# DeltaNet mixer of a two-layer DiT: loop order written as slots with TensorE's order pinned, q and k norms as per-token scales

## The chip, the core and the metric

One NeuronCore of a Trainium2 chip runs the whole program. The metric is the device time of one execution in microseconds (us).

## The reference

Two layers over 768 tokens (256 context, 512 image) of width 1024, batch 1, all in fp32. Layer 0 mixes with a gated DeltaNet, layer 1 with gated linear attention (GLA), and each has a feed-forward network with squared ReLU. Shift, scale and gate vectors come from a conditioning vector ("ada"). The change touches the DeltaNet alone:

```python
qkv = silu(short_conv(h @ w_qkv, conv_w))            # 5 taps
q = l2_normalize(q) * 128 ** -0.5 ; k = l2_normalize(k)   # per token, 8 heads of 128
# 16 value heads; per direction d (forward, backward), chunk by chunk, state s:
m = where(strict, beta_i * (k_i . k_j) * decay_ij, 0)
u, w = solve(eye + m, [v * beta, k * beta * exp(G)])
v_new = u - w @ s
o = (q * exp(G)) @ s + (q k^T * decay) @ v_new
s = s * exp(G_last) + (k * exp(G_last - G))^T @ v_new
# readout: rms_norm(o_fwd + o_bwd) * silu(z) @ w_out
```

## The kernel before, in words

Activations lie with features on the partitions and the 768 tokens along the free axis. The kernel takes chunks of 128 tokens, six in all. The eight key heads are worked one after the other; one key head with its two value heads is called a head pair here (g = 0 to 7).

**Dense products.** `dense` (line 215) multiplies a 1024x128 weight block into all tokens. Operands are split into a high and a low fp32r part, so each of the eight k steps is six matmuls: three products (`dstep`, line 208), each on 256 and on 512 columns. The weights arrive by DMA in two halves (`weights`, line 195); ScalarE casts the high part (line 204) and GpSimd subtracts the low part (line 205). A head pair has six such jobs: k, q, two v, two z. Layer 0's output product `dn_wo` has eight for its first half, inside the loop.

**Per head pair.** `conv_tile` (401) evacuates a job, applies five taps (one on ScalarE, four on VectorE, line 414) and SiLU. `l2n` (427) normalises q and k over the 128 features: a square on ScalarE, a product with a matrix of ones, Ln and Exp on ScalarE over 128x770, and a multiply on VectorE. `prep` (473) makes decay matrices E, products k k^T and k q^T, the matrices N and A (lines 487 to 494), then inverts the triangular systems: 32x32 blocks by a chain of 30 dependent pairs on VectorE (514 to 520), and larger blocks by small matmuls (`ZM`, lines 538 and 549; `LC`, line 563). `seq` (571) runs the recurrence: six steps in two directions. Each of the twelve turns has the products with S (593, 616), R on VectorE (596), U R (599), a copy x on ScalarE (601), Kt x and A x (607, 618), the new S (614) and the sum into oN. `zproj` (637) and `onorm` (651) make the gate, the output norm and the store.

**What sets the order.** The loop at lines 676 to 702 emits `prep(g+1)`, `seq(g)`, `zproj(g)`, `proj(g+2)`, `vproj(g+1)` and `onorm(g)` one after the other. The framework plans every engine's order when the program is built: an instruction goes as early as its planned inputs, buffers and place in the program allow. So matmuls of `seq(g)` and of later dense jobs stand interleaved, in an order that nobody wrote. On the chip each engine then runs its list in that order and waits on semaphores. SyncE's queue issues the loads and stores. PSUM is divided into tags: two banks "c" (`prep`), one "n", two "s" (`seq`), and three banks for dense outputs.

## Time and profile before

| what | value |
|---|---|
| median of 3 runs | 2505.73 us (2499.26 to 2512.78) |
| profiled execution | 2505.4 us |
| its span, first to last instruction | 2503.4 us |
| mean granted TensorE clock | 0.962 |

The profile is of that one execution. Busy time is the union of an engine's instructions; matmuls are pipelined and their ends are modelled, so a TensorE that shows as busy need not run at its rate. The rate is read from the starts of successive matmuls. PEld is the weight load. The clock is granted at one of two levels, 1.2 and 2.4 GHz, shown as 0.50 and 1.00, or as a mean.

### The profile page before, as it was taken

How to read it: one execution, taken by the hardware profiler on the slowest of the kernel's cores; microseconds unless marked ns; L12 is line 12 of the kernel's file. 1: busy time of each engine (PE TensorE's matmuls, PEld its weight loads, DVE VectorE, ACT ScalarE, POOL GpSimd, SP SyncE). 2: the span in 40 equal slices, each digit the busy share in tenths (PEclk: the TensorE clock that was granted, in tenths of full speed). 3: DMA queues.
4: the chain of work that ended last, by engine and by line, in shares of the span. 5: the costliest groups of instructions: out<-in, count | busy, mean ns of one | idle time of the engine just before them, and what ended most of it. 6: DMA issues, size and time to landing. Idle time of an engine off the chain costs nothing. (4 is left out here: it accounts for less than half of the span.)

```text
span 2503.4 us, 34922 instructions
## 1 busy us (share of the span) xinstructions
PE 2322.1 (93%) x12984; PEld 1939.7 (77%) x12984; DVE 1582.9 (63%) x2571; ACT 1135.1 (45%) x2053; POOL 938.0 (37%) x864
## 2 busy tenths in 40 slices
PE   7889889988999999899899999999899999899999
PEld 4668768777878878677688888888688777688887
DVE  5586796968778786439878797881575754311111
ACT  4654546373737464342431414132565644533432
POOL 1234353535344443544233333333142234244443
PEclk7988899999999999999999999999999999999999
DMA  6110010111111011266234333331111124133332
GB/s 233 49 51 30 22 51 30 51 35 51 47 34 56 30 56 37 70 231 206 81 119 131 122 127 125 120 122 60 44 44 39 52 76 131 53 98 98 96 98 98
DMA packets 107306, 206.60 MB, mean 83 GB/s; under 512 B 12032, under 2 KB 12544, under 8 KB 107136
## 3 DMA queue, kind: packets, MB, share of 16 engines
q1 hardware_dynamic: 106848, 203.31, 24.9%
q8 instruction: 103, 1.69, 0.3%
q10 hardware_dynamic: 288, 1.05, 0.1%
q14 instruction: 67, 0.55, 0.1%
HBM read 190.68 MB, written 13.63 MB: 82 GB/s over the span
## 5 line engine op out<-in xcount | busy, mean ns | idle before, releaser
L75 POOL TENSOR_TENSOR wl<-wr,wh 128x512 fp32r<-128x512 f32 x419 | 572.7, 1369 | 1076.5 <-ACT wh L204 982.9
L204 ACT CAST wh<-wr 128x512 fp32r<-128x512 f32 x452 | 279.2, 620 | 749.9 <-PE d L98 683.5
L98 PE MATMUL d<-hh,wh 128*128 128x256 f32 (+1 forms) x1856 | 595.8, 370 | 20.1 <-ACT hh L261 14.2
L98 PE MATMUL d<-hh,wl 128*128 128x256 f32 (+1 forms) x1856 | 578.7, 362 | 8.0 <-POOL wl L75 7.9
L98 PE MATMUL d<-hl,wh 128*128 128x256 f32 (+1 forms) x1856 | 582.0, 363 | 1.0 <-DVE hl L263 1.0
L98 PEld LDWEIGHTS d<-hh,wh 128*128 128x128 f32 x1856 | 354.9, 193 | 75.4 <-ACT hh L261 18.1
L98 PEld LDWEIGHTS d<-hh,wl 128*128 128x128 f32 x1856 | 352.5, 193 | 54.0 <-POOL wl L75 10.4
L98 PEld LDWEIGHTS d<-hl,wh 128*128 128x128 f32 x1856 | 353.2, 193 | 49.5 <-DVE hl L263 3.4
L75 DVE TENSOR_TENSOR avp<-avw,cB 128x512 f32<-128x512 f32 x256 | 232.4, 936 | 99.2 <-DMA avw<-ada_t 97.0
L98 PE MATMUL d<-gh,wh 128*128 128x512 f32 (+1 forms) x768 | 232.5, 357 | 0.0
L98 PE MATMUL d<-gl,wh 128*128 128x512 f32 (+1 forms) x768 | 231.0, 356 | 1.1 <-DVE gl L75 1.1
L98 PE MATMUL d<-gh,wl 128*128 128x512 f32 (+1 forms) x768 | 231.3, 356 | 0.0
L78 DVE SCALAR_TENSOR_TENSOR xT<-d,mods,xT 128x256 f32<-128x256 f32 (+1 forms) x120 | 75.6, 657 | 202.0 <-PE d L98 202.0
L98 PEld LDWEIGHTS d<-gl,wh 128*128 128x128 f32 x768 | 144.4, 188 | 24.2 <-DVE gl L75 1.7
L98 PEld LDWEIGHTS d<-gh,wh 128*128 128x128 f32 x768 | 144.4, 188 | 22.0
L98 PEld LDWEIGHTS d<-gh,wl 128*128 128x128 f32 x768 | 144.5, 188 | 21.3
L75 POOL TENSOR_TENSOR U<-Y,cm 128x256 f32<-128x256 f32 x96 | 81.1, 849 | 210.2 <-PE s L98 146.2
L75 DVE TENSOR_TENSOR gl<-ft,gh 128x768 fp32r<-128x768 f32 (+1 forms) x64 | 52.6, 822 | 168.1 <-ACT gh L773 168.1
L189 DVE TENSOR_REDUCE mods<-avp 128x1 f32<-128x1024 f32 x128 | 156.1, 1219 | 4.0
L78 DVE SCALAR_TENSOR_TENSOR cv<-rp,convw,cv 128x770 f32<-128x770 f32 x128 | 141.0, 1101 | 26.3 <-ACT cv L412 25.1
L605 POOL TENSOR_SCALAR Kt<-Kn,tailb 128x128 f32<-128x128 f32 x160 | 121.3, 770 | 80.3 <-ACT Kn L443 42.7
L98 PE MATMUL d<-oh,wh 128*128 128x256 f32 (+1 forms) x320 | 97.9, 365 | 14.1 <-ACT wh L204 6.0
(269 smaller groups left out, 3823.2 us busy)
## 6 DMA issues: line engine op xcount, KB each, us to landing
wr<-ffn SPq DMA_DIRECT2D x256, 256.0 KB, 2.8
avw<-ada_t SPq DMA_DIRECT2D x128, 256.0 KB, 3.2
aw<-ada_w SPq DMA_DIRECT2D x64, 256.0 KB, 4.1
wr<-dn_qkv SPq DMA_DIRECT2D x64, 256.0 KB, 2.8
wr<-dn_z SPq DMA_DIRECT2D x32, 256.0 KB, 2.8
wr<-dn_wo SPq DMA_DIRECT2D x32, 256.0 KB, 3.2
oD<-of SPq DMA_DIRECT2D x16, 384.0 KB, 3.6
ol<-oD SPq DMA_DIRECT2D x16, 384.0 KB, 3.5
```

Of the source, the lines that this page charges most:

```text
L75: (eng or self.dve).tensor_tensor(o, a, b, op=op)
L78: self.dve.scalar_tensor_tensor(o, a, s, b, op0=op0, op1=op1)
L98: pe.matmul(out, lhsT, rhs, start=start, stop=stop, skip_group_check=True)
L189: dve.reduce_sum(mods[:, l, part, m, s:s + 1], p, axis=mybir.AxisListType.X)
L204: act.copy(wh, r)
L605: pool.tensor_scalar(Kt[:, hh], Kn[:, c], tailb[:, c, d, r0 + hh:r0 + hh + 1], None, op0=MUL)
```

## The change

The DeltaNet loop is rewritten as Python generators that are advanced slot by slot while the program is built. In each slot, in this order: one third of a turn of `seq` (a turn is three slots: S products, R and the previous turn's Kt x and A x; U and Kt for the next turn; U R and x); one k step (six matmuls) of the dense stream; one step of every side generator (conv with one tap a slot, `prep` with one pair of the 30 a slot, norms, `onorm`, ada). All TensorE instructions of the loop are pinned to that program order; the other engines' order is still planned. Dense jobs stand in a fixed plan of six per head pair, and weights of the next half job are emitted one half job ahead. From the code: 470 slots in all, 448 of them with a dense step; 64 ahead of the first head pair, then 51, 51, 48, 48, 48, 48, 45 and 66 for head pairs 0 to 7, of which `seq` takes 37 each.

q and k are left without their norms. Per-token sums of squares come from 24 small products a head pair with two columns of ones; their scales go into A and N (`use`), Kt (`tb`), V (`sk`), and q's scale is absorbed by the output norm (`wq`). The Ln and Exp of k's norm run on 18 columns together with the output norm's. The sum of the two directions' E moves from VectorE to GpSimd; A and N become multiplications by a per-token scalar and a tile; three copies out of PSUM move from VectorE to ScalarE. S, R and x keep one buffer instead of two. N and Y have three. One U and one Kt are made a turn ahead. The loads of `dn_wo`'s input are issued before the last head pair.

The diff, cut (a line "..." marks what is left out):

```diff
-            def l2n(s, dst, extra):
-                sq = cv3.tile([P, NG], F32, name=nm("sq"), tag="c3")
-                act.activation(sq, s, AF.Square)
-                for (o, n) in ((0, 258), (258, 512)):
-                    mm(ps[:, :n], ones, sq[:, o:o + n])
-                    act.activation(sq[:, o:o + n], ps[:, :n], AF.Ln, bias=e_4eps)
-                act.activation(sq, sq, AF.Exp, scale=-0.5, bias=e_qs if extra else 0.0)
-                tt(dst, s, sq, MUL)
...
+            pin = tc.keep_in_program_order
+
+            def pmm(out, lhsT, rhs, start=True, stop=True):
+                pin(pe.matmul(out, lhsT, rhs, start=start, stop=stop, skip_group_check=True))
...
+            def norms(g, n):
+                W, dst = ready[g, "W"]
+                act.activation(W[:, 0:n], W[:, 0:n], AF.Ln)
+                sk = sp.tile([P, NCH], F32, name=nm("sk"), tag="sk", bufs=3)
+                act.activation(sk, W[:, 0:6], AF.Exp, scale=0.5)
+                act.activation(W[:, 0:n], W[:, 0:n], AF.Exp, scale=-0.5)
+                rk2 = sp.tile([P, NCH], F32, name=nm("rk"), tag="rk", bufs=3)
+                tb = sp.tile([P, NCH, 2, 2], F32, name=nm("tb"), tag="tb", bufs=3)
+                tt(rk2, W[:, 0:6], W[:, 0:6], MUL)
+                tt(tb, tailb[:, :, :, 2 * g:2 * g + 2],
+                   rk2.unsqueeze(2).unsqueeze(3).broadcast_to([P, NCH, 2, 2]), MUL)
+                ready[g, "KT"] = (dst, rk2, sk, tb)
...
+            def kq_done(g, kind):
+                def done(cv, t):
+                    while state["seqdone"] < g - 2:
+                        yield
+                    dst = hd2.tile([P, NG], F32, name=nm(kind), tag=kind)
+                    stt(dst, t, 1.0, cv, ADD, MUL)
+                    yield
+                    sq = cv
+                    act.activation(sq, dst, AF.Square)
+                    yield from idle(2)
+                    ps = psm("n")
+                    for c in range(NCH):
+                        o = cg(c)
+                        pmm(ps[:, 2 * c:2 * c + 2], sq[:, o:o + P], ones[:, 0:2])
+                    ss = ps[:, 0:2 * NCH].rearrange("p (c t) -> p c t", t=2)[:, :, 0]
+                    if kind == "KT":
+                        W = sp.tile([P, 18], F32, name=nm("W"), tag="W", bufs=2)
+                        dve.tensor_scalar(W[:, 0:6], ss, 4 * EPS, None, op0=ADD)
+                        ready[g, "W"] = (W, dst)
+                        if g < 2:
+                            norms(g, 6)
+                    else:
+                        wq = sp.tile([P, NCH], F32, name=nm("wq"), tag="wq", bufs=3)
+                        dve.tensor_scalar(wq, ss, 4 * EPS, 512 * EPS, op0=ADD, op1=MUL)
+                        ready[g, "QT"] = (dst, wq)
+                    yield
...
+                def use(c0, hh, E, A, pv, KK):
+                    rk2 = ready[g, "KT"][1]
+                    tt(N[:, c0:c0 + 2, hh], E[:, 0], E[:, 1], ADD, pool)
                     for c in range(2):
+                        stt(A[:, c].rearrange("p (d h) i -> p d h i", h=2)[:, :, hh], E[:, :, c, :], rk2[:, c0 + c:c0 + c + 1],
+                            pv[:, 1, c:c + 1, :].broadcast_to([P, 2, P]), MUL, MUL)
+                    for c in range(2):
+                        stt(N[:, c0 + c, hh], N[:, c0 + c, hh], rk2[:, c0 + c:c0 + c + 1], KK[:, c], MUL, MUL)
...
-                    Es = t2p.tile([P, 2, 2, P], F32, name=nm("Es"), tag="t2")
-                    tt(Es, E[:, 0:2], E[:, 2:4], ADD)
-                    tt(N[:, c0:c0 + 2].rearrange("p c h i -> p h c i"), Es,
-                       KK.unsqueeze(1).broadcast_to([P, 2, 2, P]), MUL)
...
                     tt(X[:, 0:k, k + 1:32], X[:, 0:k, k + 1:32], tv, ADD)
+                    if k in xb:
+                        yield
+                state["xdone"] = g
...
+                def kx(h, p2, x, Kt):
+                    step, d = divmod(h, 2)
+                    c = order[d][step]
+                    if step < 5:
+                        for hh in range(2):
+                            pmm(p2[:, hh * P:(hh + 1) * P], Kt[:, hh], x[:, hh])
+                    for hh in range(2):
+                        pmm(p2[:, 256 + hh * P:256 + (hh + 1) * P], As[c // 2][:, c % 2, 2 * d + hh, :], x[:, hh])
+                    if step < 5:
                         if step == 0:
+                            S[d] = sp.tile([P, 2 * P], F32, name=nm("S"), tag=f"S{d}", bufs=1)
+                            act.copy(S[d], p2[:, 0:256])
                         else:
                             for hh in range(2):
+                                hs = slice(hh * P, (hh + 1) * P)
...
+                nx = pre(0)
+                prev = None
+                for h in range(12):
+                    step, d = divmod(h, 2)
+                    c = order[d][step]
+                    ks = slice(cg(c), cg(c) + P)
+                    U, Kt = nx
+                    if step == 0:
+                        R = Vn[:, c]
+                    else:
+                        p1 = psm("s")
+                        pmm(p1[:, 0:256], KT[:, ks], S[d])
+                        pmm(p1[:, 256:512], QT[:, ks], S[d])
+                        R = sp.tile([P, 2, P], F32, name=nm("R"), tag="R", bufs=1)
                         for hh in range(2):
+                            stt(R[:, hh], p1[:, hh * P:(hh + 1) * P], neG[:, c, d, r0 + hh:r0 + hh + 1], Vn[:, c, hh], MUL, ADD)
+                    if prev is not None:
+                        kx(*prev)
+                    if step > 0:
+                        for hh in range(2):
+                            pq = p1[:, 256 + hh * P:256 + (hh + 1) * P]
+                            sg = neG[:, c, d, r0 + hh:r0 + hh + 1]
+                            if not done[c]:
+                                act.activation(oN[:, c, hh], pq, AF.Copy, scale=sg)
                             else:
+                                stt(oN[:, c, hh], pq, sg, oN[:, c, hh], MUL, ADD)
+                    if h == 11:
+                        state["seqdone"] = g
+                    yield
+                    nx = pre(h + 1)
+                    yield
+                    p2 = psm("s")
+                    for hh in range(2):
+                        pmm(p2[:, hh * P:(hh + 1) * P], U[:, hh], R[:, hh])
+                    x = sp.tile([P, 2, P], F32, name=nm("xv"), tag="xv", bufs=1)
+                    act.copy(x, h2(p2[:, 0:256]))
+                    prev = (h, p2, x, Kt)
+                    yield
+                kx(*prev)
+                yield
...
+            plan = [[job("k", 0), job("q", 0), job("v", 0, 0), job("v", 0, 1), job("k", 1), job("q", 1), job("z", 0, 0), job("z", 0, 1)]]
+            for g in range(6):
+                plan.append([job("v", g + 1, 0), job("v", g + 1, 1), job("k", g + 2), job("q", g + 2), job("z", g + 1, 0), job("z", g + 1, 1)])
+            plan.append([job("v", 7, 0), job("v", 7, 1), job("z", 7, 0), job("z", 7, 1)])
+            plan.append([job("w", mt) for mt in range(8)])
...
+            def stream():
...
+                    while state["evac"] < n:
+                        yield False
+                    while onS and not state["sfree"]:
+                        yield False
+                    outs = [psm("s")[:, 0:256] if onS else ps256(), ps512()]
+                    for hf in range(2):
+                        wh, wl = nw
+                        if hf == 0:
+                            nw = weights(wd, 1, 2)
+                        elif n + 1 < len(jobs):
+                            nw = weights(jobs[n + 1][0], 0, 2)
+                        for k4 in range(4):
+                            k = hf * 4 + k4
+                            xh, xl = rh(k)
+                            for (w, x) in ((wh, xh), (wh, xl), (wl, xh)):
+                                for (o, nn), ps in zip(SPL_ALL, outs):
+                                    pmm(ps[:, :nn], w[:, k4, :], x[:, o:o + nn], start=k == 0 and w is wh and x is xh,
+                                        stop=k == 7 and w is wl)
+                            if k == 7:
+                                side.insert(0, fin(outs))
+                            yield True
...
+                while True:
+                    if g >= 0 and sq_ is None and state["prepped"] >= g and (g, "V", 0) in ready and (g, "V", 1) in ready and (g, "Kn") in ready:
+                        sq_ = seq(g)
+                        state["sfree"] = False
+                    if sq_ is not None and sq_ != 1:
+                        try:
+                            next(sq_)
+                        except StopIteration:
+                            sq_ = 1
+                            state["sfree"] = True
+                            side.append(onorm(g))
+                            if g == 6:
+                                side.append(wo_in())
+                            if g < 7:
+                                side.append(kn_nat(g + 1))
+                    if left and next(dense_s):
+                        left -= 1
+                    state["left"] = left
+                    if started < 7 and state["xdone"] >= started and state["seqdone"] >= started - 1:
+                        started += 1
+                        side.append(prep(started, xmid if started == 1 else xslow))
+                    advance()
```

## Rows read from the trace of the kernel before

**Rows 1.** The page: busy time of TensorE over the span; the granted clock in 40 slices.

```profile
PE 2322.1 (93%) x12984; PEld 1939.7 (77%) x12984; DVE 1582.9 (63%) x2571; ACT 1135.1 (45%) x2053; POOL 938.0 (37%) x864
...
PEclk7988899999999999999999999999999999999999
```

**Rows 2.** Busy time by stretch (us): window, its length, busy (instructions) per engine, clock, DMA.

```profile
63.00:207.00 144.00, 120.33 (x665) 100.40 (x664) 93.28 (x145) 82.49 (x144) 36.00 (x33) 0.86 0.14 46
207.00:330.00 123.00, 109.85 (x650) 92.75 (x649) 98.62 (x196) 70.20 (x151) 55.54 (x62) 0.92 0.08 26
674.00:791.00 117.00, 109.59 (x684) 93.19 (x683) 94.02 (x189) 64.30 (x132) 51.17 (x56) 0.96 0.14 43
731.00:761.00 30.00, 27.80 (x166) 25.24 (x166) 16.04 (x27) 18.51 (x33) 6.57 (x8) 0.83 0.06 19
908.00:1016.00 108.00, 98.82 (x595) 83.46 (x595) 81.20 (x179) 44.73 (x95) 45.73 (x55) 0.93 0.12 42
1016.00:1136.00 120.00, 104.64 (x569) 84.25 (x568) 49.20 (x94) 42.66 (x77) 60.98 (x50) 0.96 0.53 174
1300.00:1350.00 50.00, 50.00 (x285) 43.38 (x284) 43.44 (x50) 7.45 (x12) 14.82 (x12) 1.00 0.39 122
```

**Rows 3.** Timeline of ScalarE: first x copies of head pair 4; start, us, instruction.

```profile
674.37 0.66 ACT L601 COPY xv<-s 128x256 f32<-128x256 f32 x2
```

**Rows 4.** Waits of TensorE (PE, PEld) in 674 to 791 us: total, times, longest.

```profile
PE s L98 <- DVE R L78: 4.9, 4, 2.1
PE d L98 <- POOL wl L75: 1.3, 1, 1.3
...
PEld s L98 <- DVE R L78: 7.0, 7, 2.5
...
PEld s L98 <- ACT xv L601: 1.2, 4, 0.5
```

**Rows 5.** Timeline of TensorE near 733 and 743 us: dense pairs at two clocks.

```profile
732.27 0.52 PE L98 MATMUL d<-hh,wh 128*128 128x256 f32 x2
732.62 0.52 PE L98 MATMUL d<-hl,wh 128*128 128x256 f32 x2
...
743.34 0.84 PE L98 MATMUL d<-hh,wh 128*128 128x256 f32 x2
743.98 0.84 PE L98 MATMUL d<-hl,wh 128*128 128x256 f32 x2
```

**Rows 6.** Timeline of TensorE: starts of small products and of what follows them.

```profile
757.82 0.65 PE L98 MATMUL s<-S,KT 128*128 128x256 f32 x2
758.12 0.59 PE L98 MATMUL d<-hh,wl 128*128 128x512 f32 x1
...
759.01 1.45 PE L98 MATMUL c<-LC,N 128*128 128x64 f32 x12
760.27 0.48 PE L98 MATMUL d<-hl,wh 128*128 128x512 f32 x1
...
762.55 0.71 PE L98 MATMUL s<-xv,A 128*128 128x128 f32 x4
763.01 0.48 PE L98 MATMUL d<-hh,wl 128*128 128x512 f32 x1
```

**Rows 7.** Groups of VectorE in 674 to 791 us: count, busy us, mean ns, idle before.

```profile
L78 DVE SCALAR_TENSOR_TENSOR R<-s,neG,Vn 128x128 f32<-128x128 f32 x20 | 6.6, 344 | 0.2
...
L75 DVE TENSOR_TENSOR A<-E,c 128x512 f32<-128x512 f32 x6 | 4.1, 678 | 0.0
...
L75 DVE TENSOR_TENSOR N<-Es,KK 128x512 f32<-128x512 f32 x3 | 2.6, 856 | 0.0
...
L75 DVE TENSOR_TENSOR Es<-E 128x512 f32<-128x512 f32 x3 | 2.1, 686 | 0.1
...
L75 DVE TENSOR_TENSOR KK<-c,cm 128x256 f32<-128x256 f32 x3 | 1.3, 419 | 0.0
```

**Rows 8.** Group of GpSimd in 674 to 791 us: the U masks.

```profile
L75 POOL TENSOR_TENSOR U<-Y,cm 128x256 f32<-128x256 f32 x12 | 10.3, 862 | 18.4 <-PE s L98 14.0 <-ACT Y L566 4.2
```

**Rows 9.** Timeline near 491 us: VectorE beside a GpSimd add.

```profile
490.90 0.26 DVE L75 TENSOR_TENSOR tmp<-X 128x108 f32<-128x108 f32 x1
...
491.20 1.28 POOL L75 TENSOR_TENSOR wl<-wr,wh 128x512 fp32r<-128x512 f32 x1
491.34 1.27 DVE L75 TENSOR_TENSOR X<-X,tmp 128x108 f32<-128x108 f32 x1
```

## What I expect the change to do

> **What bounds the kernel now.** I read the page first. TensorE is busy 93% of the span and every other engine 63% or less, and its clock falls below full only in the first half, most of all in slices 1 to 4 [rows 1]. So the question is TensorE, in the DeltaNet part. Next I read the busy time by stretch, cut where `seq` of a head pair makes its first x, for pair 4 at 674 us [rows 3]; the other cuts lie at 207, 330, 441, 559, 791, 908 and 1016. Ahead of the first head pair stand 144 us (63 to 207), head pairs 0 to 5 take 701 us (207 to 908, 117 of them the one at 674), pair 6 takes 108 and pair 7 with the output product 120 [rows 2]. That is 1073 of the 2503 us; the change reaches nothing else.
>
> How far is TensorE from its rate there? Busy time can't tell. Between 1300 and 1350 us, with dense products alone and full clock, 285 matmuls take 50.00 us [rows 2], 0.1754 us each, so a dense slot of six costs 1.053 us. The small products are priced by starts in a stretch at full clock [rows 6]: two S records (one product) 0.30 us; four records of x (two products) 0.46 us, so 0.23 a product; twelve LC records 1.26 us, 0.105 each. A steady head pair holds 48 slots (50.5 us); 80 products of 128 columns in `seq` and `prep` (18.4); 20 with S (6.0); 96 ZM and LC records (10.1); 24 decay products at the 256-column share of the dense rate, about 0.12 (2.9); 30 transposes at about 0.11, near an LC record (3.3); sums for the norms (2.5). The sum is 93.7 us of own work, in a period of 117. About 23 us are lost.
>
> Where to? The clock is 0.96 in that period, so it lost 0.04 of 117, 4.7 us. All of it lies between 731 and 761, where the mean is 0.83 [rows 2] and successive dense pairs start 0.64 us apart instead of 0.35 [rows 5]: the lower level, 1.2 GHz. Just ahead of it TensorE waited for R and had ZM products with little beside them. The waits: 4.9 us of matmul idle behind R, 1.3 behind a low weight part [rows 4]; idle in all is 117 minus 109.59, 7.4 us [rows 2]. The other 11 us are weight loads that could not run ahead because the instruction behind them was waiting (7.0 us of load idle behind R alone [rows 4]), and first records of small groups. VectorE is the next engine: 94.02 of 117 [rows 2]. R waits because VectorE's list holds longer work ahead of it.
>
> **The change part by part.**
>
> *TensorE's own work.* The same dense jobs and the same small products. The norm's product with ones (258 and 512 columns, two records each) becomes 24 records for k and q together, at 0.105 also 2.5 us. Nothing gained. The 16 ada units move among earlier slots; the same work.
>
> *Order.* In the new order a turn's S products are followed by R, which TensorE needs two slots later; x is needed one slot later, S three. A slot is 93.7 / 48 = 1.95 us of TensorE. So R has nearly 4 us where the longest wait for it now is 2.5 [rows 4]. ZM and LC products stand between dense steps, so the stretch with the low clock should vanish: minus 4.7 us. I take half of the remaining 18 us back and a little more, as pinning also fixes every short wait: x (one buffer now) sits on ScalarE behind up to 3 us of E or conv, the products k k^T now share the two "s" banks with `seq`, and whatever is behind on TensorE's list waits with them. That leaves 11 us lost and a period of 104.5. Bounds: 97 (3 us lost, as in the stretch of dense products alone where nothing waits) and 117 (all of it lost again in other waits), beyond that under the rivals. I take the middle, since two of three causes are removed by construction and the third is not.
>
> *VectorE.* Removed per head pair: A 4.1, N 2.6, Es 2.1 [rows 7], two 770-wide multiplies and three kinds of PSUM copies, which I count only as a margin. Added: 12 A pieces of 256 at about KK's 0.42 (5.0), 12 N pieces of 128 at no more than R's 0.344 (4.1) [rows 7], and some eight tiny ones. So 94.0 − 8.8 + 9.1 and about 1 for the tiny ones, less the margin: 91 to 96, taken as 93. Against 104.5 that is 0.89 of the period, hidden, but without much room; it becomes the bound if the period falls under 96.
>
> *GpSimd* gains six adds of 256 at U's 0.862 us [rows 8], 5.2 us: 51.17 becomes 56 of 104.5, hidden behind TensorE. But one row shows a price on VectorE: an X step of 108 elements that started 0.14 us after a GpSimd add took 1.27 us and ended 0.13 after it, where its twin just ahead took 0.26 [rows 9]. By that row each new add could hold VectorE for at most 0.86 us, 5.2 us a head pair; VectorE would stand at 98 of 104.5. The sum goes without it, since 98 is still less. The Trainium skill, "SBUF — State Buffer", section "Who interferes with whom", says that a VectorE instruction with two SBUF inputs contends with a GpSimd one that reads SBUF, and that the later one blocks fully. The trace shows it for this one pair, and the rule, which speaks against this move, makes of it a cost of every add that an X step follows: the upper 98 instead of the lower 93, and then the time of the first rival below, 2408, is nearer than the forecast leaves it.
>
> *ScalarE* takes the copies but sheds the 770-wide Ln and Exp: about 64 of 117 before [rows 2] and hardly more after; hidden, except as x's queue above.
>
> *DMA.* Same bytes. Weights are issued half a job earlier on SyncE's queue; ada's loads (two a unit) share its three buffers, so a late ada product can hold a weight load behind it there. The queue's engines are 0.14 busy [rows 2] and today a low part cost TensorE 1.3 us in the period [rows 4]; between nothing and twice that, taken as equal, inside the 11 us. The eight loads of the output product move ahead of the last pair, past the weight loads of pair 7: hidden, and the casts of its first tile cost some 3 us of TensorE at the start, as the old buffers free only then.
>
> *Sum.* Head pairs 0 to 5: six periods of 104.5 and the six extra slots of pairs 0 and 1 (6 to 8 us, with ada): 635 against 701, minus 66 (bounds: 590 to 701). Ahead of them: 64 slots (67.4) and about 27 us of first `prep`, norms, transposes and ada on TensorE, 94; VectorE's chain of the first inversion starts only after two jobs, so 111, against 144: minus 33 (bounds 100 to 144). Pair 6: 32 dense slots (33.7), `seq` (21.6), ZM and LC (10), the rest 3, so 68, but 13 slots have no dense step, so waits show: 86 against 108, minus 22 (bounds 75 to 108). Pair 7: 64 dense slots (67.4), `seq` (21.6), transposes, so 91; with the first-tile wait and losses 101 against 120, minus 19 (bounds 95 to 120). Together minus 140. The profiled execution is 2505.4 us (span 2503.4), within 0.4 us of the median. 2505.4 − 140 = **2365 us**. All bounds at their best give 2292, at their worst no change. About 0.5% (12.5 us) is what a measurement of this kernel can tell from no change.
>
> **The rivals.**
>
> *VectorE becomes the bound.* Its list is at 93 to 98 us and in order. In slots with an E/A/N piece or a 2 us transpose it has more than twice TensorE's work, so R and S come late and periods settle near 110: its 98 and half of the 23 us that it idles today (117 − 94). For: R is already the largest wait [rows 4], and [rows 9]. Against: 0.80 busy now, R has longer to come. Six periods 5.5 longer than forecast and the first part 10 longer: 2365 + 33 + 10 = 2408. Chance 0.20.
>
> *Nearly own work.* The waits go altogether: period 98, and 102, 78 and 96 in the other parts: 2365 − 39 − 9 − 8 − 5 = about 2304. For: the stretch of dense products alone has no idle. Against: small groups cost more than their own price behind any wait. Chance 0.14.
>
> *The pinned order is a chain of short waits: slower.* Now, when R is late, a planned dense product stands before it; pinned, the whole list waits. Each turn has three handoffs (R, x, S), 36 a head pair, and x has one slot and one buffer behind ScalarE's bursts. It decides from (117 − 93.7) / 36 = 0.65 us lost at each handoff; at 0.9 us the period is 126, six periods add 54, pairs 6 and 7 about 10, the first part still saves 20: about 2550. For: fixed order, single buffers. Against: x costs 1.2 us of load idle in a period today [rows 4]. Chance 0.07.
>
> *The change does no more than the planner did.* TensorE's waits change place, the low clock stays, and the first part's gain is within the noise: 2505. For: before, too, dense and `seq` products stand interleaved [rows 5, 6]. Against: the low clock and R's waits are of that very order. Chance 0.05.
>
> **How the numbers follow.** Forecast 0.54, with its own range of 2325 to 2395; VectorE 0.20; near own work 0.14; slower 0.07; no change 0.05. Faster by over 0.5%: 0.54 + 0.20 + 0.14 = 0.88; same 0.05; slower 0.07. The range reaches down to the best bounds, 2290, and up past the VectorE case to 2455, where losses have eaten some two thirds of the gain. It leaves out the slower case, no change, and the tails.
>
> **What would show it.** Right: `seq` of pairs 2 to 5 about 104 us apart, clock 1.00 there, load idle behind R below 3 us a period, VectorE near 0.89 of it, same count of dense matmuls. Wrong: periods of 110 or more with waits of TensorE on R and S (VectorE) or on x (ScalarE); dense products waiting for low weight parts; a first part still near 140; a clock still under 1.00 in the loop.

## The result, and the profile after

The changed kernel takes 2521.05 us (median of 6 runs, 2514.53 to 2528.06) against 2504.55 for the kernel before (6 runs, 2499.26 to 2512.78): ratio 1.0066, 95% interval 1.0039 to 1.0093. It is slower by 0.7%, where 2365 us was forecast. Its profiled execution is 2514.5 us with a span of 2512.8, 9.4 more than the span before. The page's busy line and clock line, to be held against [rows 1]:

```profile
PE 2282.8 (91%) x13112; PEld 1956.0 (78%) x13112; DVE 1576.4 (63%) x2655; ACT 1097.9 (44%) x2097; POOL 970.2 (39%) x908
...
PEclk8889998899999998997999999999899999899999
```

The busy times by stretch, cut as before where a head pair makes its first x; the last line is the first stretch of the program that the change does not touch:

```profile
63.00:221.00 158.00, 132.96 (x833) 115.05 (x834) 108.68 (x215) 78.62 (x173) 52.41 (x54) 0.88 0.17 52
...
703.00:820.00 117.00, 104.11 (x663) 92.86 (x662) 95.51 (x197) 58.91 (x134) 56.10 (x62) 0.96 0.11 35
820.00:935.00 115.00, 101.04 (x663) 90.01 (x663) 94.32 (x197) 58.83 (x134) 56.22 (x62) 0.99 0.11 35
935.00:1034.00 99.00, 79.31 (x492) 69.06 (x492) 73.92 (x152) 47.78 (x98) 47.62 (x48) 0.93 0.19 62
1034.00:1134.00 100.00, 91.50 (x560) 80.68 (x558) 29.43 (x77) 34.04 (x68) 44.66 (x46) 0.99 0.42 144
1134.00:1236.00 102.00, 77.38 (x397) 65.00 (x398) 92.82 (x118) 28.96 (x43) 34.92 (x22) 0.83 0.51 165
```

Against [rows 2]: the first part grew from 144 us to 158, head pairs 0 to 5 from 701 to 714 (221 to 935), and pairs 6 and 7 with the output product shrank from 228 to 199. The loop's last copy of a `dn_wo` product out of PSUM (yp) starts at 1133.8 us; before it was 1134.5. So the loop as a whole gained nothing, and the 10 us come after it: from the last yp to the end 1379.0 us, before 1368.9. They lie in the second half of `dn_wo`, whose last product starts 90.8 us after that yp, before 78.2; what follows takes 1288.2 us, before 1290.7. In the same 102 us behind the loop the kernel before made 452 matmuls at clock 0.93:

```profile
1134.00:1236.00 102.00, 87.07 (x452) 71.80 (x450) 94.79 (x120) 33.00 (x52) 36.92 (x23) 0.93 0.42 140
```

Within the loop, gains and losses lie apart. Pairs 0 and 1 and then pairs 6 and 7, cut at each pair's first product with U; before, then after:

```profile
206.10:429.90 223.80, 201.68 (x1219) 169.10 (x1217) 174.58 (x360) 120.22 (x247) 97.15 (x105) 0.94 0.11 35
898.20:1134.50 236.30, 211.91 (x1217) 175.13 (x1215) 136.32 (x278) 96.34 (x192) 115.39 (x114) 0.95 0.33 109
```

```profile
219.50:467.50 248.00, 220.31 (x1449) 195.00 (x1448) 179.15 (x378) 120.32 (x274) 110.66 (x126) 0.91 0.15 49
934.30:1133.80 199.50, 171.52 (x1055) 150.44 (x1053) 103.85 (x229) 81.71 (x165) 92.08 (x94) 0.96 0.30 103
```

Up to pair 0's first product the new kernel is 13.4 us later, pairs 0 and 1 take 24.2 us more with 230 more TensorE records, pairs 2 to 5 take 1.5 us less, and pairs 6 and 7 take 36.8 us less with 162 fewer records. A large part of the gain at the end is work that now stands earlier.

What TensorE waits for in the steady pair (703 to 820), against [rows 4]:

```profile
PE s L405 <- DVE oN L75: 4.0, 2, 2.6
PE n L805 <- DVE of L78: 3.7, 2, 2.5
PE s L405 <- ACT oN L748: 2.5, 2, 1.4
PE s L405 <- DVE oN L78: 1.3, 1, 1.3
PE s L405 <- DVE R L78: 0.8, 1, 0.8
```

The wait for R fell from 4.9 us to 0.8, as forecast. In its place TensorE now waits for PSUM: U R, and once the first product with S, needs an s bank that the sums into oN of the turn before still read (4.0 + 2.5 + 1.3 = 7.8 us), and the readout's transposes need the one n bank that `of` still reads. The releaser is mostly the same engine as before, VectorE, at a later answer of the turn. TensorE's busy time did fall, from 109.59 us in the pair of [rows 2] to 104.11 and 101.04 here, close to its own work; but idle rose from 7.4 us to 12.9 (117 - 104.11) and 14.0 (115 - 101.04), and the period stayed.

Behind the loop, TensorE's timeline at the hand-over to the second half of `dn_wo` (start, length, idle before and what ended it); first after, then before:

```profile
1127.05 0.51 PE L405 MATMUL d<-oh,wl 128*128 128x256 f32 x2
1148.22 1.01 PE L98 MATMUL d<-oh,wh 128*128 128x256 f32 x2 [20.67 <-ACT wh L204]
```

```profile
1133.90 0.51 PE L98 MATMUL d<-oh,wl 128*128 128x256 f32 x2
1139.74 1.01 PE L98 MATMUL d<-oh,wh 128*128 128x256 f32 x2 [5.33 <-ACT wh L204]
```

TensorE ends the loop 7 us earlier and starts again 8 us later. VectorE's and SyncE's timelines show what is late: pair 7's last readout piece, and behind its store the loads of the second input and then of the weights:

```profile
1110.90 0.48 DVE L78 SCALAR_TENSOR_TENSOR of<-n,small,sz 128x256 f32<-128x256 f32 x1
```

```profile
1124.76 3.91 SPq L960 DMA_DIRECT2D ol<-oD  x3
1130.58 2.61 SPq L960 DMA_DIRECT2D ol<-oD  x2
1142.15 0.90 SPq L198 DMA_DIRECT2D wr<-dn_wo  x2
```

Before, the last `of` stood 53 us ahead of the loop's end; now it stands 16 us ahead.

### The profile page after: what moved, and what is told of

Its sections match the earlier page's. It is cut to its first block, busy times and chain, and to the rows that moved or that the text cites. A ratio compares the mean times of both kernels' runs of the same rounds, so it can differ in the third digit from the quotient of the medians.

```text
span 2512.8 us, 35426 instructions
## 1 busy us (share of the span) xinstructions
PE 2282.8 (91%) x13112; PEld 1956.0 (78%) x13112; DVE 1576.4 (63%) x2655; ACT 1097.9 (44%) x2097; POOL 970.2 (39%) x908
## 5 line engine op out<-in xcount | busy, mean ns | idle before, releaser
L98 PE MATMUL d<-hh,wh 128*128 128x256 f32 (+1 forms) x1088 | 339.0, 364 | 14.9 <-ACT hh L261 14.2
L98 PE MATMUL d<-hh,wl 128*128 128x256 f32 (+1 forms) x1088 | 335.5, 360 | 5.5 <-POOL wl L75 5.5
L98 PE MATMUL d<-hl,wh 128*128 128x256 f32 (+1 forms) x1088 | 335.3, 361 | 1.0 <-DVE hl L263 1.0
L75 DVE TENSOR_TENSOR avp<-avw,cB 128x512 f32<-128x512 f32 x256 | 216.0, 870 | 99.6 <-DMA avw<-ada_t 97.2
L98 PEld LDWEIGHTS d<-hh,wh 128*128 128x128 f32 x1088 | 207.2, 192 | 50.5 <-ACT hh L261 18.7
L98 PEld LDWEIGHTS d<-hh,wl 128*128 128x128 f32 x1088 | 206.6, 191 | 36.4 <-POOL wl L75 6.5
L98 PEld LDWEIGHTS d<-hl,wh 128*128 128x128 f32 x1088 | 207.2, 191 | 33.4 <-DVE hl L263 3.0
L405 PE MATMUL d<-hh,wh 128*128 128x256 f32 (+1 forms) x704 | 217.7, 384 | 10.3 <-ACT rp L427 10.3
L405 PE MATMUL d<-hh,wl 128*128 128x256 f32 (+1 forms) x704 | 196.7, 355 | 0.0
L405 PE MATMUL d<-hl,wh 128*128 128x256 f32 (+1 forms) x704 | 196.6, 354 | 0.0
L78 DVE SCALAR_TENSOR_TENSOR cv<-rp,convw,cv 128x770 f32<-128x770 f32 x128 | 150.7, 1177 | 25.5 <-ACT cv L432 24.9
L699 POOL TENSOR_SCALAR Kt<-Kn,tb 128x128 f32<-128x128 f32 x160 | 114.0, 725 | 121.1 <-PE s L405 66.6
```

The source lines that it names most:

```text
L75: (eng or self.dve).tensor_tensor(o, a, b, op=op)
L78: self.dve.scalar_tensor_tensor(o, a, s, b, op0=op0, op1=op1)
L98: pe.matmul(out, lhsT, rhs, start=start, stop=stop, skip_group_check=True)
L405: pin(pe.matmul(out, lhsT, rhs, start=start, stop=stop, skip_group_check=True))
L699: pool.tensor_scalar(Kt[:, hh], Kn[:, c], tb[:, c, d, hh:hh + 1], None, op0=MUL)
```

## The experiments

Each ratio is to the kernel before on the same chip, with its 95% interval. "Pairs 2 to 5" is the mean spacing of four steady pairs, taken from each pair's first product with U; "first" is when pair 0 makes that product. Runs without a ratio are one execution.

| run | median us | ratio | first | pairs 2 to 5 |
|---|---|---|---|---|
| before | 2504.55 | 1 | 206.1 | 117.1 |
| changed | 2521.05 | 1.0066 [1.0039, 1.0093] | 219.5 | 116.7 |
| e1 TensorE free | 2454.38 | 0.9836 [0.9790, 0.9881] | 204.7 | 109.6 |
| e2 three s banks | 2548.58 | 1.0203 [1.0170, 1.0235] | 225.8 | 123.7 |
| e3 no recurrence | 2479.86 | | 219.1 | 111.1 |
| e4 light VectorE | 2427.91 | | 199.6 | 107.5 |
| e5 oN first | 2515.94 | 1.0074 [1.0049, 1.0099] | 220.7 | 116.3 |
| e6 e3 and e4 | 2421.64 | | 200.0 | 107.9 |
| e7 e1, old norms | 2477.01 | 0.9905 [0.9874, 0.9935] | 198.7 | 114.2 |
| e8 e1, weights early | 2455.91 | 0.9832 [0.9810, 0.9854] | 202.0 | 110.4 |
| e9 dense, recurrence pinned | 2503.61 | 1.0000 [0.9977, 1.0023] | 211.3 | 116.9 |
| e10 e1, pair 7 fast | 2444.82 | 0.9778 [0.9733, 0.9823] | 196.8 | 109.6 |
| e11 e8, loads on GpSimd's queue | 2449.30 | 0.9791 [0.9757, 0.9825] | 201.6 | 113.0 |
| e12 E add on VectorE | 2531.27 | 1.0109 [1.0077, 1.0140] | 227.9 | 117.0 |
| e13 dense free | 2467.95 | 0.9862 [0.9832, 0.9892] | 202.7 | 112.9 |
| e14 dense alone pinned | 2500.03 | 0.9991 [0.9972, 1.0009] | 214.0 | 116.6 |
| e15 VectorE pinned instead | 2505.13 | 1.0016 [0.9993, 1.0039] | 214.5 | 116.9 |
| e16 pinned, pair 7 fast | 2505.44 | 1.0008 [0.9990, 1.0025] | 224.8 | 116.1 |
| e17 before, light VectorE | 2430.99 | | 145.7 | 114.1 |
| e18 e10, jobs off VectorE | 2476.59 | 0.9901 [0.9867, 0.9935] | 213.5 | 112.7 |

**Is it the pinned order?** e1:

```diff
-            pin = tc.keep_in_program_order
+            pin = lambda i: i
```

> The changed kernel with the same program text but TensorE's instructions no longer pinned: the planner orders them as it did before. Theory A, the pinned order (TensorE's list stands still behind short waits, about 14 us in a steady head pair of 117): the planner puts dense products into those waits, steady periods fall to about 106 and the time by 50 us or more, to about 2465. Theory B, VectorE answers too late whatever the order: same within 15 us, 2505 to 2535. Theory C, TensorE's own work was priced too low (about 110 a pair, not 94): same within 15 us as well, since the work is the same. If pinning was a gain that something else in the change ate: slower than 2550.

Measured 2454.38, 67 us under the changed kernel by the medians (the ratios, each to the kernel before on its own chip, make it 58) and faster than before: near theory A's time, though pairs fall to 109.6 and not to 106. Its steady pair:

```profile
652.80:761.50 108.70, 100.21 (x663) 88.83 (x662) 95.65 (x197) 59.12 (x133) 56.27 (x62) 1.00 0.11 37
```

TensorE's and VectorE's busy times are near those of the pinned kernel; idle is 8.5 us instead of 13 to 14, and the clock is full. Of the 63.6 us by which the loop is shorter than the pinned one in these two traces, 14.8 lie ahead of pair 0's first product, 19.8 in pairs 0 and 1, 28.4 in pairs 2 to 5; 41.6 of them are less idle time of TensorE, 22.0 less busy time. The wait for oN is still there (7.5 us); those for `of`, Kn and R are nearly gone:

```profile
PE s L405 <- DVE oN L75: 4.5, 3, 1.8
PE s L405 <- ACT oN L748: 3.0, 2, 1.6
PE n L805 <- DVE of L78: 0.5, 2, 0.3
```

**Is it the s banks?** e2:

```diff
-            ps_scope(dn, True, 2)
+            ps_scope(dn, True, 1, 3)    # one c bank, three s banks
```

> The changed kernel with three PSUM banks for the recurrence ('s') and one for prep ('c') in place of two and two. The profile's waits of TensorE for an s bank that an oN operation still reads are 7.8 us of the steady pair at 820. Theory A in its form 'banks': these waits go, steady periods fall by 6 to 8 us, 45 to 55 in all, less what one c bank costs in the first part: about 2475. Theory B, VectorE's queue: the same lateness shows as waits for R and S instead, periods within 3 us of 117, time 2505 to 2530. Theory C: the same, 2510 to 2525.

The waits for oN went, and others came; the pair from 843 to 968 us:

```profile
PE s L405 <- DVE R L78: 6.7, 5, 2.2
...
PE c L405 <- ACT N L662: 2.1, 2, 1.0
PE c L405 <- ACT Y L662: 2.1, 2, 1.0
```

TensorE waits 6.7 us for R where it waited for oN. That is theory B's picture. Its numbers failed, though: pairs take 123.7 and the program 2548.58, where B had at most 120 and 2530, and waits for the single c bank came with it. So the s banks chose which late answer of VectorE shows; a third s bank without giving up a c bank was not tried.

**How much is TensorE's own work, how much VectorE's lateness?** e3, e4 and e6, in which e6 joins the two edits:

```diff
-                        pmm(p1[:, 0:256], KT[:, ks], S[d])
+                        pmm(p1[:, 0:256], KT[:, ks], Vn[:, c].rearrange("p h v -> p (h v)"))   # e3, e6; QT alike
+                        R = Vn[:, c]                    # and x = Vn[:, c]; S and oN left out
-                for n, tap in enumerate((0, 1, 3, 4)):
+                for n, tap in enumerate((0,)):          # e4, e6
                 for k in range(1, 31):
+                    if k > 1: ... continue              # e4, e6
```

> All TensorE instructions of the changed kernel in the same pinned order, but the recurrence's operands are tiles that are long ready (V in place of R, S and x), and R, S, x and the sums into oN are left out on VectorE and ScalarE: TensorE waits for nothing in a turn but U and Kt. What it computes is not the DeltaNet. Theories A and B: steady periods fall to 95 to 101, as own work is 94. Theory C: they stay at 108 or more with TensorE busy throughout.

> The changed kernel with three of the four VectorE conv taps and 29 of the 30 steps of the 32x32 inversion left out (its output is not the DeltaNet), in the same slots: VectorE falls from 95 to about 53 us of a steady period, TensorE's list is the same. Theory B, VectorE's queue makes R, S and the bank releases late: idle of TensorE behind VectorE falls from 9 us to under 3, periods to 105 or less. Theory A in its form 'banks': the waits for oN come from the order of short operations in one turn and stay over 5 us; periods 112 or more. Theory C: periods 110 or more with TensorE busy throughout.

> e3 and e4 together (no recurrence on VectorE and ScalarE, one conv tap on VectorE, no chain of the 32x32 inversion; not the DeltaNet): TensorE's pinned list with next to nothing to wait for. Theory C, own work was priced too low: steady periods of 99 to 103 with TensorE busy for nearly all of it. If own work is the 94 us of the prediction: 97 or less.

One steady pair each of e3, e4 and e6:

```profile
681.30:794.00 112.70, 101.05 (x663) 91.01 (x662) 78.21 (x139) 51.50 (x109) 56.39 (x63) 0.97 0.11 36
```

```profile
755.50:863.10 107.60, 99.82 (x664) 90.09 (x663) 55.56 (x127) 59.04 (x133) 49.68 (x62) 0.98 0.12 37
```

```profile
641.50:749.60 108.10, 99.64 (x664) 90.02 (x663) 40.32 (x69) 51.51 (x109) 51.51 (x63) 0.98 0.11 37
```

In e3 no turn waits, yet the pair takes 112.7, where theories A and B had 95 to 101: a transpose of V now waits 4.6 us for VectorE's SiLU multiply (tn). With 40 us less on VectorE (e4) the pair takes about 107.5, between theory A's 112 and B's 105, with 2.9 us left behind VectorE; taking the recurrence away as well (e6) gives nothing more. There TensorE is busy for 99.64 us, as theory C has it, but the period is nobody's: 8.3 us of idle stay behind `of` (3.7), rp (3.2; the copy of a finished job out of PSUM), Kn (k transposed) and Y, answers that are late in the pinned order whatever VectorE has to do. So the list costs just under 100 us, not 94, and VectorE's lateness about 9 of the 117 (116.7 - 107.5). Freeing the order gives 7.1 by itself (e1, 109.6); whether the two add up was not tried.

**Does a better order within the turn help?** e5:

```diff
 def kx(h, p2, x, Kt):
-    S[d] update ; oN -= p2
+    oN -= p2 ; S[d] update
-                        yield
+                        yield from idle(2)    # ahead of each n<-osq group
```

> The changed kernel, pinned, with two things moved in the program text: in a turn the subtraction into oN stands ahead of the update of S (oN's end frees the s bank that U R wants two slots later, S is wanted six slots later), and the transposes of the readout (n<-osq) come one slot later each. Theory A, short waits that a better written order avoids: the steady pair's waits behind oN (7.8 us) fall below 4 and those behind 'of' (3.7) below 1; period 117 to about 110, time about 35 us shorter than the changed kernel's, near 2480. Theory B, VectorE's list is late as a whole: the lateness turns up behind R or S, periods 115 or more, time within 10 us of the changed kernel's.

No gain (ratio 1.0074). The lateness passed to S, in the pair from 816 us on:

```profile
PE s L405 <- DVE S L78: 4.4, 2, 2.6
PE s L405 <- ACT oN L747: 3.0, 2, 1.8
PE n L804 <- DVE of L78: 2.1, 2, 1.3
```

**Norms or program order?** e7 puts the norms of the kernel before into e1:

```diff
-    pmm(ps[:, 2 * c:2 * c + 2], sq[:, o:o + P], ones[:, 0:2])   # six, then W, rk, sk, tb, wq
+    pmm(ps[:, :n], ones, sq[:, o:o + n]) ; Ln ; Exp ; tt(dst, t, sq, MUL)
```

> e1 (unpinned) with the norms of the kernel before: products with a 128-wide matrix of ones, Ln and Exp over 128x770, q and k multiplied by them, A and N without scales in one operation each per value head, no scale at V. If the gain of e1 over the kernel before comes from the norms: it is lost, 2485 or more. If it comes from the slots' program order and the moved jobs: within 12 us of e1, 2442 to 2466.

Between the two: 0.9905 against e1's 0.9836, with intervals that overlap a little. The norms as scales are worth some 17 us (0.0069 of 2500), and the rest of the change (the new program order, planned freely, and the moved jobs) about 24 (0.0095).

**What holds TensorE behind the loop?** e8, e10, e11 (on e1) and e16 (on the changed kernel):

```diff
+        wo0 = [weights(I["dn_wo"][0, 1], hf, 2) for hf in range(2)]   # e8, e11: ahead of the ol loads
-                nc.sync.dma_start(t, oD[8 + k])
+                nc.gpsimd.dma_start(t, oD[8 + k])                     # e11
                             next(sq_)
+                            if g == 7:
+                                next(sq_)                             # e10, e16
```

> e1 (unpinned) with the loads and casts of the first block of dn_wo's second half issued ahead of the loads of its input and of the ada rows that follow the loop. If SyncE's queue order made the rest of the program 10 us longer than in the kernel before (1380 against 1369 us from the last yp on): 2442 to 2448. If the loads of its input set that: within 4 us of e1's 2454.

> e1 (unpinned) with the last head pair's recurrence advanced two steps a slot instead of one, so that its readout is stored earlier. If TensorE's 20 us gap between the loop and the second half of dn_wo (5.7 us in the kernel before) comes from pair 7's readout, which now ends some 17 us ahead of the loop's end instead of 53: the gap falls under 10 us and the time by 6 to 14, to 2440 to 2448. If the gap comes from the weights or the ada rows in SyncE's queue: gap and time as in e1, 2454 within 5; slower if the recurrence stalls the last pair.

> e8 with the eight loads of dn_wo's second input issued on GpSimd's queue, so that they do not stand behind the stores of the last readout on SyncE's. If SyncE's order holds them (six of the eight were stored long before): the gap closes, time 2440 to 2448. If memory of the loop that comes free late, or the last two stores, hold them: within 5 us of 2455.

> The changed kernel, pinned, with the last pair's recurrence advanced two steps a slot, as in e10. If the late readout of pair 7 costs the pinned kernel its 21 us gap after the loop (5.7 before) and the low clock behind it: the gap falls under 8 us and the time by 8 to 20, to 2501 to 2513, equal to the kernel before. If the pinned list stalls in the denser recurrence: 2515 or more.

e8: the gap between the last product of the loop and the next one, 19.9 us of idle in e1, is gone, but the hundredth product of the second half starts 43.2 us after the last yp, e1's 39.4, and the time is e1's: with the first weights there, low parts of the input are late (4.2 us in four waits), and then a later weight block (7.2 us in one). e10: 1.2 us of idle at the hand-over, last `of` 43 us ahead of the loop's last product instead of 17, ratio 0.9778. From the last yp to the last matmul it takes 1365.4 us, e1 1375.9, the kernel before 1364.9: the 10 us are back. Its timeline at the hand-over:

```profile
1065.22 0.51 PE L405 MATMUL d<-oh,wl 128*128 128x256 f32 x2
1066.96 0.62 PE L98 MATMUL d<-oh,wh 128*128 128x256 f32 x2 [1.24 <-ACT wh L204]
```

e11 gives 0.9791, under e1 but within its interval; the queue order is a part at most. e16 does to the pinned kernel what e10 does to e1: 1.0 us of idle at the hand-over, last `of` 41 us ahead, ratio 1.0008 against 1.0066, intervals apart. The second half of `dn_wo` ends 74.2 us after the last yp in e10 and in e16, 95.9 in e1 and 90.8 in the changed kernel. So the late readout of the last pair is what turns an equal result into a slower one.

**Does the E add on GpSimd hold VectorE?** e12:

```diff
-                    tt(N[:, c0:c0 + 2, hh], E[:, 0], E[:, 1], ADD, pool)
+                    tt(N[:, c0:c0 + 2, hh], E[:, 0], E[:, 1], ADD)
```

> The changed kernel, pinned, with the six adds of E on VectorE again. If GpSimd's adds hold VectorE while they run (by the X step that ended with one: up to 5.2 us a head pair): VectorE's other groups shrink by more than the 2.8 us that the adds cost there, the time falls by 10 to 25 us to about 2500. If not: VectorE 98 of a steady pair, time the same or up to 15 us longer, 2520 to 2536.

Groups of VectorE in a steady pair of e12 (count, busy, mean ns); then the same two of the changed kernel:

```profile
L78 DVE SCALAR_TENSOR_TENSOR cv<-rp,convw,cv 128x770 f32<-128x770 f32 x16 | 18.8, 1174 | 3.0 <-ACT cv L432 3.0
...
L78 DVE SCALAR_TENSOR_TENSOR N<-N,rk,KK 128x128 f32<-128x128 f32 x12 | 4.2, 391 | 0.0
L75 DVE TENSOR_TENSOR N<-E 128x256 f32<-128x256 f32 x6 | 3.2, 532 | 0.0
```

```profile
L78 DVE SCALAR_TENSOR_TENSOR cv<-rp,convw,cv 128x770 f32<-128x770 f32 x16 | 20.0, 1252 | 3.0 <-ACT cv L432 3.0
...
L78 DVE SCALAR_TENSOR_TENSOR N<-N,rk,KK 128x128 f32<-128x128 f32 x12 | 5.0, 457 | 0.0
```

The adds cost VectorE 3.2 us, and the neighbours give back 1.2 and 0.8; both groups are shorter on average in e12 in each of pairs 2 to 5. So GpSimd's adds do hold VectorE, by some 2 us a pair, not 5.2, and moving them off it is right by 1 us; with them back the time is not shorter but some 10 us longer (1.0109 against 1.0066). By the Trainium skill, "SBUF — State Buffer", "Who interferes with whom", a VectorE instruction with two SBUF inputs and a GpSimd one that reads SBUF contend, and issue order decides which of them blocks. The 2 us agree with that rule in sign; the upper end that [rows 9] gave for every add is not reached.

**Which part of the list must be free?** e9 pins dense and recurrence only, e13 everything but dense, e14 dense only, e15 VectorE instead of TensorE:

```diff
-                pmm(...)           # in prep, kq_done, nat, adag, onorm: e9 ; in stream: e13 ; all but stream: e14
+                mm(...)
-    dve.op(...)                    # in the loop: e15, with TensorE free
+    pin(dve.op(...))
```

> The changed kernel with only the dense stream and the recurrence pinned; the side products (decay, k k^T, sums of squares, ZM, LC, all transposes, ada) are placed by the planner. If pinning costs its 67 us (2521 against e1's 2454) because a side product whose operand is late stands in the one list (in the steady pair at 820 transposes waited 4.8 us for 'of' and Kn): 2475 or less. If it costs them in the recurrence and the dense products: 2505 or more.

> The changed kernel with everything of TensorE's loop pinned but the dense stream, which the planner places. If the pinned list loses because dense products cannot move into a wait for the recurrence: most of the 67 us comes back, 2475 or less. If the order of the recurrence and the side products against one another, or VectorE's order, is the cause: 2500 or more.

> The changed kernel with the dense stream alone pinned (its products keep their order among themselves); recurrence and side products are free. If what matters is that dense and recurrence can move against one another: as e1, 2450 to 2465. If the planner's gain in e1 came from reordering the dense products among themselves (their accumulation steps run out of order there): 2490 or more.

> TensorE free as in e1, VectorE's instructions of the loop pinned to program order. If VectorE's order, which the planner changed along with TensorE's in e1, makes the 67 us: time goes to 2500 or more. If TensorE's order makes it: 2445 to 2470.

Freeing the side products alone gives 17 us (e9, 1.0000), all outside the steady pairs: the waits for `of` and Kn that I had read as the cost of pinning are not it. Freeing the dense products alone gives 53 of the 67 us by the medians (e13; 51 of 58 by the ratios). Pinning them alone takes most of it away again (e14), and so does pinning VectorE with TensorE free (e15). The steady pairs follow, 112.9 for e13, 116.6 to 116.9 for the others, but they hold only 15 of e13's 53 us; 40 lie ahead of pair 2. A reading that fits all four is that the gain needs two lists that are planned together, with the dense products to fill in; no run shows it by itself. By e14's expectation its 2500 says that the planner gained by reordering the dense products among themselves. The steady pairs hardly show that: of 263 steps from one dense record to the next, 239 follow the program's order in the changed kernel and 230 in e1. Why e14, where the recurrence may move between dense products, does not get the gain stays open.

**Was the kernel before any different?** e17 applies e4's two edits to the kernel before, e18 tries a small relief of VectorE on e10:

```diff
-                    tt(ts[hh], oN[:, :, hh, :], ss..., MUL)        # e18
+                    act.activation(ts[hh][:, c, :], oN[:, c, hh, :], AF.Copy, scale=ss[:, hh, c:c + 1])
-                    tt(Y..., Z1..., Z2..., ADD)
+                    tt(Y..., Z1..., Z2..., ADD, pool)
```

> The kernel before with three of the four VectorE conv taps and 29 of the 30 steps of the 32x32 inversion left out (its output is not the DeltaNet), as e4 did to the changed kernel. If the order of TensorE's list was what cost 23 us a pair: steady periods stay above 112. If VectorE's late answers and own work above 94 made the 117: periods fall to about 107, as in e4, and the time by 60 us or more.

> e10 with two small jobs moved off VectorE: the output norm's scaling to ScalarE (twelve activations in place of two 768-wide multiplies, 1.9 us) and the four additions of the diagonal blocks of Y to GpSimd (2.2 us). If VectorE's lateness still sets the steady pair (42 us taken off it gave 8 to 10 a pair in e4, so 4 off give about 1): 2436 to 2442, 3 to 9 under e10. If GpSimd's longer additions delay Y and hold VectorE: equal or up to 10 slower.

With VectorE light the kernel before takes 2430.99 us and the changed one 2427.91, one execution each: with quick answers the two orders are worth about the same in total. The expectation of 107 a pair failed: pairs of 114.1 are on the side that was to blame TensorE's order. That of 60 us held, but 60 of the 72 us lie ahead of pair 0's first product (206.1 to 145.7) and only 3 a pair in pairs 2 to 5. So a light VectorE takes 9 us off the steady pair of the changed kernel and 3 off that of the kernel before. e18 lost 32 us to e10 where a gain was expected; idle behind oN in its pair at 660 is 9.3 us (6.0 + 2.8 + 0.5). Which of the two edits did it, and by what, was not tried.

## Why the prediction was wrong

**The step that failed** is "I take half of the remaining 18 us back and a little more, as pinning also fixes every short wait", which made a period of 104.5 out of 117. Measured: 114.4 to 120.3 in pairs 2 to 5. Against the terms of the sum: pairs 0 to 5 minus 66 forecast, plus 13 measured; the part ahead of them minus 33 and plus 14; pairs 6 and 7 minus 41 and minus 29; behind the loop nothing and plus 10. Three things lay under the step that failed.

*Own work was priced too low, by about 6 us.* Two S records were priced at 0.30 us by the start of what follows them [rows 6]. But that follower, a 512-column dense product, then shows 0.59 us where it shows 0.48 behind other groups: a start alone can be early. In the changed kernel S products stand together, and the starts give the price (18 such pairs of records in the pair from 820 us on, nearly all 0.43):

```profile
833.07 0.70 PE L405 MATMUL s<-S,KT 128*128 128x256 f32 x2 [1.29 <-DVE oN L78]
833.60 0.59 PE L405 MATMUL s<-S,QT 128*128 128x256 f32 x2
834.03 0.61 PE L405 MATMUL s<-xv,Kt 128*128 128x128 f32 x4
```

That is 0.43 a product, 20 x 0.13 = 2.6 us more a pair. And the first dense pair behind a small group takes 0.43 us, the next ones 0.35:

```profile
902.48 0.60 PE L405 MATMUL d<-hh,wh 128*128 128x256 f32 x2
902.91 0.51 PE L405 MATMUL d<-hl,wh 128*128 128x256 f32 x2
903.26 0.51 PE L405 MATMUL d<-hh,wl 128*128 128x256 f32 x2
```

A small group stands ahead of dense products 39 times in that pair; 39 x 0.083, the mean difference, is 3.2 us, which the prediction had booked among the losses ("first records of small groups"). 93.7 + 2.6 + 3.2 = 99.5; e6 has 99.64 busy, e1 100.21. The best bound of 97 was below the list's own work.

*The idle time rose where it was to fall.* The busy part of the loss went, as forecast: 101 to 104 us of busy time are the list's own work and a little clock. But the prediction gave R "nearly 4 us" and took that for the whole turn. R did come in time (0.8 us). A turn needs four answers, though, R, x, the sums that empty the bank, and S, from lists that also hold 1.25 us conv taps and 2 us transposes, and in a fixed list whichever stood last stopped everything: oN in the changed kernel, R in e2, S in e5. Less work on VectorE (e4, idle 7.8 us) or a free order (e1, 8.5 us) shortens it; the one other fixed order that was tried (e5) did not. The rival "VectorE becomes the bound" had the mechanism, but its period of 110 needed answers that come sooner than these.

*Pinning costs instead of giving.* The same program with TensorE free is 67 us faster by the medians (e1). The rival "chain of short waits: slower", given 0.07, had the sign and half of the mechanism: the whole list stands behind one late answer. Its place was wrong (x hardly shows; it is the bank behind oN), and its threshold of 0.65 us a handoff was not reached: 14 us idle over 36 handoffs is 0.39. The period did not grow (116.7 against 117.1): with own work of 99.5 the same arithmetic gives 0.48 us a handoff, idle and low clock together. The kernel became slower in pairs 0 and 1, ahead of them, and behind the loop.

**The low clock did not vanish.** Between 63 us and the last yp the granted clock stood at its lower level for 136 us in all, before for 116, in e1 for 82. TensorE's idle time in the same stretch goes with it in these three (132, 104 and 90 us), but not in every run: e13 has 89 idle and 116 at the low level, e7 107 and 61. What set the clock stays open. Nor did it fall "only in the first half": behind the last yp the kernel before has 45 us at the lower level, the changed one 79.

**The first part**: 111 forecast, 158 measured. TensorE shows 833 records there instead of 665: more of `prep` and of ada now stands in it (decay products with RA 24 against 13, ada 112 against 64), which the sum booked later, and products wait in the list for rp, the squares of the norms, tn and A (up to 4.7 us each). Freeing TensorE gives 15 us of it, lightening VectorE 20.

**Pairs 6 and 7**: the cut at 1016 us was late, as pair 7's first x before is at 1005.5; together they took 228 us and were forecast at 187. They take 199, the one gain in the loop. `dn_wo`'s products now stand beside the whole of pair 7's recurrence, as forecast (before, beside 46 of its 64 us), but part of the gain is the work that moved ahead of pair 2, where it costs as much: 37.6 us there against 36.8 here, by the first products with U. But the prediction wrote that the change "reaches nothing else". It takes away what stood between pair 7's readout and the second half of `dn_wo`, and TensorE waits 20.67 us there. What would be late next was not asked at the loop's end.

**What held**: VectorE's busy time (91 to 96 forecast, 94 to 95.5 measured), with A and N pieces dearer than forecast (0.47 and 0.46 us against 0.42 and 0.34); GpSimd's 56; no wait for weights in the steady pair.

## What to carry to other kernels

Before a new order is credited with the time that an engine loses, take that engine's own work from products of one kind, and ask of every answer that it waits for, not of the longest wait alone, when it comes. Pinning one engine fixes what is waited for; the planner, free on the same program, was 67 us better, and letting the big independent products move was enough for 53 of them. And follow the last stage of a rewritten loop into the code behind it: work moved beside the last iteration can delay what the next stage reads (e10 repairs this, and at 2445 us, ratio 0.9778, is the fastest version here that leaves nothing out).

## What had not been expected

A product's price read from the next start can be too low when what follows is of another kind (0.30 against 0.43 us). More banks for the late stage made the kernel slower by 1.4% by the ratios (e2 against the changed kernel): the wait moved to R, and new waits for the c bank came. And moving 4 us of work off VectorE cost 32 us (e18 against e10), which no busy time of the engines foretells.
